# Norm means from float32r pairs, and squares of the first feed-forward nets kept for VectorE

## The chip, the cores and the metric

One Trainium2 chip, one of its cores. The metric is the device time of one execution in microseconds (us): the median of several runs, 2788.34 for the kernel before.

## The reference, cut to what matters

Two blocks run one after the other on x of 512 tokens by 1024 features, all in float32. The first has two layers of an attention mixer and a feed-forward net with a squared relu; the second has a state space block, two gated convolutional nets ("second nets" here) and an attention of another kind. What the change touches is the norm ahead of each of these parts:

```python
def rmsnorm(x, g):
    xf = x.astype(jnp.float32)
    y = xf * lax.rsqrt(jnp.mean(xf * xf, axis=-1, keepdims=True) + EPS)
    return (y * g.astype(jnp.float32)).astype(x.dtype)
...
    for l in range(DEPTH):
        u = rmsnorm(x, pre_mix_g[l])
        m = token_mixer(u, ...)
        x = x + rmsnorm(m, post_mix_g[l])
        h = rmsnorm(x, pre_ffn_g[l]) @ w_ffn_up[l]
        f = jnp.square(jax.nn.relu(h)) @ w_ffn_down[l]
        x = x + rmsnorm(f, post_ffn_g[l])
```

Inside each mixer two more such norms are taken, over 384 and over 256 features.

## The kernel before, in words

**Layout.** Activations lie with features on the 128 partitions and the 512 tokens along the columns, so x is eight tiles of 128 x 512. A float32 value that goes into a product is held as two float32r parts, hi (rounded, written by ScalarE) and lo (the rest, written by VectorE); a product of two such values is three float32r products (hi by hi, hi by lo, lo by hi), `mm3`. Weights come from DRAM in units of 128 x 1024 (SP's queue, `raw`), and are split into `wh` (ScalarE, L230) and `wl` (VectorE, L233). Four buffers hold each of raw, wh and wl. Three short-lived pools matter: 16 tiles of 128 x 512 (s2), 24 of twice that (s4), and 8 banks of PSUM.

**A norm.** The gain is multiplied into x while it is split (xg, L571 and L360), and the division by the root of the mean square is put off: it is multiplied in when a product is taken out of PSUM. The mean square over features is a sum over partitions and tiles. `sq_acc` (L395) squares each tile on ScalarE (L402) and adds the squares into `acc`: for half-width columns on GpSimd (L411, L414), for whole ones on GpSimd too except the first and the last. The eighth tile's square stays apart as `sq`. `mean_mm` (L416) multiplies a matrix of equal constants by acc, and by sq where there is one, in float32, and `rstd` makes the factor from it: three steps on ScalarE (L368, L376, L377), two on VectorE (L384, L388).

**A boundary.** `boundary` (L546) ends a part: for one half of the columns after the other it multiplies the part's result (pn, L567), adds it to x (xr, L568), makes xg's two parts and squares x. The products of the next part begin meanwhile: `lead_group` (L424) runs its first three or four output tiles together, one tile of x after the other, again half by half. It ends with pre(), which issues the mean and the factor; four slots later the tiles are taken out of PSUM by evac. Behind the lead group the other tiles follow one by one (24 products each), for the first nets eight up-tiles and then eight down-tiles, four times over. The norm factor `rr` is first used by `ht` (L591) in a first net, by `z` (L811) in a mixer, by `u` (L1390) in the state space block. There u goes to DRAM and comes back in another order as U, and `vps` are the products with U.

**Order.** The program is a list of closures (`plan`), in the state space block and the attentions by an order written out by hand. `later(n, fn)` issues fn once products of n slots more have been issued; a slot is 512 columns in float32r, and a float32 product counts four. From the instructions so issued a scheduler makes the order of each engine's queue, by priority (earlier issued first) among those that are ready; `pin` keeps an instruction behind all that its engine has been given. Around a lead group the weight splits are pinned: splits of new units wait until 22 closures of the lead group are through, and are pinned for 30 more.

**Which means there are.** Over the whole width twelve: one ahead of each of the two mixers, the two first nets, the state space block, the two second nets and the last attention, and two inside each mixer. Of these the first five named have acc and sq, the others only acc. Ten more run over half the columns, inside the four boundaries and at the end of the kernel.

Of the kernel before, what the change touches and what calls it, by code (L numbers as in the profile page):

```python
# [6 lines left out]
F32 = mybir.dt.float32  # L7
F32R = mybir.dt.float32r
AF = mybir.ActivationFunctionType
ALU = mybir.AluOpType  # L10
AX = mybir.AxisListType

D = 1024
# [94 lines left out]
class Kernel:  # L108
# [21 lines left out]
    LAG = 3  # L130
    LD = 2
# [28 lines left out]
    # ---------------------------------------------------------------- tiles  # L160
# [20 lines left out]
    # -------------------------------------------------------------- weights  # L181
# [14 lines left out]
    def split_early(self, h):  # L196
        """half of the first three units"""
# [40 lines left out]
    def weight(self, u, a, m):  # L238
        """columns a .. a + m of both parts of a unit"""
        hi, lo, w = self.whl[u]  # L240
        i, o = divmod(a, w)
        return hi[i][:, o:o + m], lo[i][:, o:o + m]
# [50 lines left out]
    def later(self, n, fn):  # L293
        """emit fn once n more slots (of 512 columns) of products have been emitted"""
        self.queue.append((self.clock + n, fn))
# [10 lines left out]
    # ------------------------------------------------------------- matmuls  # L306
# [7 lines left out]
    def pin(self, ins):  # L314
        """ins stays behind what its engine has been given so far"""
        self.tc.keep_in_program_order(ins)

    def mm_tok(self, out, x, t, u, a, first, last, n=256):
        """out [128 tokens of tile t, n] += x[:, tokens].T @ W[columns a .. a + n of a unit], in three float32r passes"""
# [14 lines left out]
    def mm3(self, ps, u, k0, nk, kt, m0, m, xs, first, last, ncol=None, cols=ALL):  # L334
        """ps += W[k-tiles, cols].T @ x over nk k-tiles, in three float32r passes."""
# [10 lines left out]
    def split(self, dst, src, scale=None, gain=None):  # L346
        """dst[:,0] + dst[:,1] = src (times scale or a per-partition gain)."""
# [14 lines left out]
    def ln(self, out, in_, load=True, **kw):  # L362
        """Ln from the table set that has Exp too; load: unless it is there already."""
# [6 lines left out]
    def rstd_a(self, v, l=None, cols=ALL, load=True):  # L370
        """v: mean square, the same in all the rows it is used for (PSUM)."""
# [8 lines left out]
    def rstd_b(self, vyq, name="r", cols=ALL, r=None, pin=False):  # L380
        """one Newton step; the result is -2 / sqrt(v + eps): y * ((v + eps) * y * y - 3)"""
# [12 lines left out]
    # ------------------------------------------------------- generic phases  # L394
    def sq_acc(self, st, src, i, n, scale=1.0, cols=ALL, pin=False, one=False):  # L395
        """running sum of squares over tiles; the last stays apart."""
# [26 lines left out]

    def lead_group(self, units, n, xs, evac, st, ones="ones_d", pre=None, mid=None, feed=None):  # L424
        """The first n output tiles k-tile by k-tile, so that the products start with the first tile of x;
        mid: the two halves of the columns one after the other, with mid() once the first has begun."""
        pss = []

        def emit(k, cols, last):
# [4 lines left out]
            if last and k == KT - 1:  # L434
                if pre is not None:
                    pre()
                    self.later(4, lambda: [evac(j, pss[j]) for j in range(n)])
# [34 lines left out]
    def half_tiles(self, units, xs, nk, evac, js, fin):  # L472
        """the last output tiles, the two halves of the columns one after the other; fin() in the second"""
# [24 lines left out]
    # ================================================================ setup  # L498
# [37 lines left out]
    def begin_norm(self, gain, xs, st):  # L536
        """split x * gain, and start the sum of squares of x: a closure for each tile."""
# [8 lines left out]
    def boundary(self, f, st, gain, nxt, res):  # L546
        """x += the norm of f; then begin_norm of the next norm; the closures for the two halves of the columns."""
# [13 lines left out]
        def tile(h, i):  # L561
            cols = HALVES[h]
            xs = res["xs"]
            if i < KT:
# [7 lines left out]
                self.sq_acc(res["st"], x, i, KT, cols=cols)  # L572
# [4 lines left out]
    # ================================================================= FFN  # L577
    def ffn1(self, l, xs, st, nxt, mid, bg=None, last=(), feed=None):
# [7 lines left out]
        def pre():  # L586
            st["r"] = self.rstd(self.mean_mm(st, self.const("ones_d")), "rr", load=False)

        def up(j, ps):
            t = self.s2("ht")  # L590
# [52 lines left out]
    # =============================================================== mixer  # L643
# [9 lines left out]
    def head_norm(self, z, gain, then, n1, n2):  # L653
        """rms norm over the 64 rows of each head, times gain; then(result)."""
# [17 lines left out]
    def v_tiles(self, vf, vst):  # L672
        """v feature-major [two heads of 64, tokens] -> vst [token, tile, head, (hi | lo)]."""
# [8 lines left out]
    def stack(self, dst, src, scale=None):  # L682
        """src [two heads of 64, S] -> dst[h] with hi and lo stacked on the partitions."""
# [11 lines left out]
    def dup(self, dst, src, scale=None):  # L695
        """src [two heads of 64, S] -> dst[h] [128, (hi, lo), S], each on both halves of the partitions."""
# [13 lines left out]
    def softmax_ops(self, name, qk, vst, ydst, spill=None):  # L710
        """The parts of a softmax attention over 8 heads in blocks of 128 queries, by name; a block (h, qt) is 4 h + qt.
        q: scores, e: exponentials, n: division by the sum, t: transposes, p: product with the values, two blocks at once.
        qk(h, qt, ps): scores. vst(h): [128, 4, 128] (hi | lo). ydst: pairs of heads -> hi/lo tiles."""
# [69 lines left out]
    def chunks(self, unit, xs, nk, evac, j, n, m0=0, ncol=None, k0=0):  # L783
        """one output tile as n closures, for use between other work."""
# [14 lines left out]
    def mixer(self, l, xs, st, nxt, mid, feed=None):  # L799
# [6 lines left out]
        def pre():  # L806
            st["r"] = self.rstd(self.mean_mm(st, self.const("ones_d")), "rr", load=False)
# [59 lines left out]
        def ev_c(which, n):  # L867
            def f(j, ps):
# [3 lines left out]
                if j == n - 1:  # L872
                    self.later(18, mean)

            def mean():
                a = self.rstd_a(self.mean_mm(cst[which], self.const("ones_" + which)))
# [16 lines left out]
        def kr_mm():  # L893
            """the products of both parts of w_kr with hi in one pass, one below the other"""
# [26 lines left out]
        # ---- grouped-query attention  # L921
# [1135 lines left out]
```

## Time and profile before

| | us |
|---|---|
| median of three runs | 2788.34 (2786.98 to 2790.88) |
| the profiled execution, first to last instruction | 2786.1 |
| TensorE busy | 2722.6 |
| VectorE busy | 1846.5 |
| ScalarE busy | 1305.1 |
| GpSimd busy | 293.4 |

The profiled execution is known by its span alone; 2.2 us lie between it and the median of the runs. TensorE's matmuls are pipelined and their ends are modelled, so its busy time is an upper bound of what it must spend. PE is TensorE's matmul and PEld its weight load, DVE is VectorE, ACT ScalarE, POOL GpSimd. A row that begins with a time gives start, length, engine, line, operation, the tile written and those read, and shapes; in brackets stands how long the engine had been idle, and who ended it. The mean granted clock of TensorE is 0.989 of its full speed over the span.

### The profile page before, as it was taken

Reading aid. Unit: us, or ns where it says so; the run is one execution under the profiler, and the core shown is the slowest. Engines: PE = TensorE matmul, PEld = TensorE weight load, DVE = VectorE, ACT = ScalarE, POOL = GpSimd, SP = SyncE. Lnnn points to the kernel's source line nnn. Section 1 sums busy time; section 2 is a strip of 40 time slices with the busy share of each in tenths; the row PEclk is TensorE's granted clock in tenths of the full one; section 3 lists DMA queues with packets and bytes.
Section 4 is the critical chain, followed back from the end, with each engine's and each line's share of the span. In section 5 each row is a group of like instructions: output and inputs, shape, how many; then the busy total and the mean of one; then the engine's idle time right before and its main releaser. Section 6 shows DMA issues by size and latency. Waiting matters only on the chain.

```text
span 2786.1 us, 35356 instructions
## 1 busy us (share of the span) xinstructions
PE 2722.6 (98%) x13470; PEld 2268.2 (81%) x13470; DVE 1846.5 (66%) x2963; ACT 1305.1 (47%) x2204; POOL 293.4 (11%) x311
## 2 busy tenths in 40 slices
PE   8999999999999999999999989999999999999998
PEld 6888888888878888888887887888887888888887
DVE  7889863444687996787745784656466667574654
ACT  6567553333465664532334214423236888542333
POOL 1000020000210101121002000101012111110101
PEclk9999999999999999999999879999999999999999
DMA  5323333333232334354445623233324223233331
GB/s 206 116 79 91 121 119 97 95 98 98 96 109 86 93 95 161 110 190 153 137 123 180 183 88 117 91 99 98 99 85 131 68 69 103 84 98 99 98 92 61
DMA packets 122651, 307.47 MB, mean 110 GB/s; under 512 B 35824, under 2 KB 42736, under 8 KB 122352
## 3 DMA queue, kind: packets, MB, share of 16 engines
q1 hardware_dynamic: 109424, 291.57, 32.7%
q10 hardware_dynamic: 10624, 8.39, 1.0%
q0 software_dynamic: 2432, 5.25, 0.9%
q8 instruction: 106, 1.74, 0.3%
q14 instruction: 65, 0.53, 0.1%
HBM read 260.59 MB, written 41.68 MB: 108 GB/s over the span
## 4 chain that ended last, share of the span: by engine, by line
PE 58%; DVE 5%; ACT 1%; issue 1%; DMA 0%; POOL 0%; SPq 0%; DVEq 0%; ACTq 0%; POOLq 0%
PE mm L312 49%; PE z L312 3%; PE yps L312 2%; PE o L312 1%; PE s L312 1%; PE vps L312 1%; DVE xg L360 0%; DVE wl L233 0%; PE gps L312 0%; PE pT L328 0%; DVE pn L567 0%; PE mean L312 0%; DVE xr L568 0%; DVE VS L1431 0%; PE gps L328 0%
## 5 line engine op out<-in xcount | busy, mean ns | idle before, releaser
L312 PE MATMUL mm<-xg,wh 128*128 128x512 f32 (+1 forms) x4080 | 1227.5, 383 | 26.6 <-DVE xg L360 15.5
L312 PEld LDWEIGHTS mm<-xg,wh 128*128 128x128 f32 x4080 | 745.4, 188 | 188.0 <-DVE xg L360 24.6
L230 ACT ACTIVATE wh<-raw 128x1024 fp32r<-128x1024 f32 (+2 forms) x417 | 431.1, 1039 | 830.0 <-PE mm L312 527.5
L312 PE MATMUL mm<-xg,wl 128*128 128x512 f32 (+1 forms) x2024 | 759.5, 378 | 0.0
L233 DVE TENSOR_TENSOR wl<-raw,wh 128x1024 fp32r<-128x1024 f32 (+2 forms) x417 | 531.3, 1278 | 161.9 <-ACT wh L230 156.7
L312 PE MATMUL mm<-hid,wh 128*128 128x512 f32 (+1 forms) x1816 | 539.1, 380 | 0.7 <-DVE hid L357 0.4
L312 PEld LDWEIGHTS mm<-xg,wl 128*128 128x128 f32 x2024 | 381.7, 189 | 71.6 <-issue 0.2
L312 PEld LDWEIGHTS mm<-hid,wh 128*128 128x128 f32 x1816 | 335.0, 188 | 67.0 <-DVE hid L357 1.2
L312 PE MATMUL mm<-hid,wl 128*128 128x512 f32 (+1 forms) x908 | 343.9, 379 | 0.0
L312 PE MATMUL mm<-yhl,wh 128*128 128x512 f32 x640 | 207.3, 403 | 8.7 <-ACT yhl L1494 4.7
L414 POOL TENSOR_TENSOR acc<-acc,sq 128x256 f32<-128x256 f32 (+1 forms) x90 | 106.6, 1185 | 953.1 <-ACT sq L402 952.5
L312 PEld LDWEIGHTS mm<-hid,wl 128*128 128x128 f32 x908 | 170.8, 188 | 31.8
L312 PEld LDWEIGHTS mm<-yhl,wh 128*128 128x128 f32 x640 | 120.1, 192 | 34.6 <-DVE yhl L1495 5.7
L1582 POOL TENSOR_TENSOR gt<-gt,cv 128x512 f32<-128x512 f32 x44 | 74.9, 1703 | 592.7 <-ACT wh L230 471.1
L312 PE MATMUL mm<-yhl,wl 128*128 128x512 f32 x320 | 127.1, 397 | 0.0
L591 DVE SCALAR_TENSOR_TENSOR ht<-mm,rr 128x512 f32<-128x512 f32 x64 | 43.8, 690 | 117.1 <-PE mm L312 116.8
L1590 DVE SCALAR_TENSOR_TENSOR xr<-mm,xr 128x512 f32<-128x512 f32 (+1 forms) x50 | 33.5, 670 | 125.3 <-PE mm L312 125.3
L607 DVE TENSOR_TENSOR part<-part,mm 128x512 f32<-128x512 f32 (+1 forms) x52 | 33.5, 644 | 113.9 <-PE mm L312 113.8
L1570 DVE SCALAR_TENSOR_TENSOR gt<-mm,rr 128x512 f32<-128x512 f32 x88 | 60.6, 690 | 69.6 <-PE mm L312 69.5
L722 DVE TENSOR_REDUCE nm<-s 128x1 f32<-128x512 f32 x128 | 86.4, 680 | 20.8 <-PE s L312 20.4
L749 ACT ACTIVATE pt<-pT 128x512 fp32r<-128x512 f32 x128 | 74.6, 594 | 46.2 <-PE pT L328 45.0
L729 ACT ACTIVATE p<-s,nm 128x512 f32<-128x512 f32 x128 | 87.1, 684 | 11.0 <-DVE nm L722 8.9
(297 smaller groups left out, 3463.5 us busy)
## 6 DMA issues: line engine op xcount, KB each, us to landing
raw<-in_w_up SPq DMA_DIRECT2D x152, 512.0 KB, 3.6
raw<-in_w_down SPq DMA_DIRECT2D x96, 512.0 KB, 3.5
raw<-in_w_in SPq DMA_DIRECT2D x51, 512.0 KB, 3.6
xd<-xr SPq DMA_DIRECT2D x16, 512.0 KB, 2.8
gd<-z SPq DMA_DIRECT2D x32, 256.0 KB, 2.2
g<-gd SPq DMA_DIRECT2D x32, 256.0 KB, 3.9
raw<-in_w_o SPq DMA_DIRECT2D x16, 512.0 KB, 3.6
raw<-in_w_glu SPq DMA_DIRECT2D x16, 512.0 KB, 4.3
```

Source lines behind the costliest of these rows:

```text
L230: ins = self.nc.scalar.activation(h, x, AF.Copy)
L233: ins = lo_engine.tensor_tensor(l, x, h.bitcast(F32), ALU.subtract)
L312: return self.nc.tensor.matmul(out, lhsT, rhs, **kw)
L414: eng.tensor_tensor(st["acc"][:, cols], st["acc"][:, cols], sq[:, cols], ALU.add)
L591: nc.vector.scalar_tensor_tensor(t, ps, 0.0, st["r"], op0=ALU.max, op1=ALU.mult)
L607: nc.vector.tensor_tensor(p, p, ps[:, cols], ALU.add)
L722: nc.vector.tensor_reduce(nm, ps, AX.X, ALU.max, negate=True)
L729: nc.scalar.activation(p, ps, AF.Exp, bias=nm, accum_out=sm)
L749: nc.scalar.activation(hi[:, :, q0:q0 + 128], v, AF.Copy)
L1570: v.scalar_tensor_tensor(t, ps, -0.5, st["r"], op0=ALU.mult, op1=ALU.mult)
L1582: nc.gpsimd.tensor_tensor(t, t, sg.pop(n), ALU.mult)
L1590: v.scalar_tensor_tensor(x, ps[:, cols], 0.5, x, op0=ALU.mult, op1=ALU.add)
```

## The change

1. `sum_split` and `mean_r` are new. The first completes acc on VectorE (adding sq, or the kept squares), scales it by -1/n and splits it into a float32r pair (ScalarE, then VectorE). The second multiplies the pair by a float32r matrix of -1: two products.
2. Seven of the eight norms ahead of a part, and the four inside the mixers, use them. The last attention, the boundaries' own means and the end of the kernel keep the float32 form.
3. At the end of a lead group `sum_split` is issued at once, the mean 10 slots later, or 32 in the first nets, and evac 4 slots after that. Tiles of a first net that finish before the factor is issued wait in a list.
4. In the two boundaries in front of a first net (keep=True) `square` keeps all eight squares, two in s2 tiles and six in three s4 tiles; nothing is added on GpSimd there. `sum_split` adds them on VectorE over all 512 columns.

```diff
+    PRE = 10
+    PRE2 = 32
...
+    def sum_split(self, st, n):
+        v = self.nc.vector
+        if "sqs" in st:
+            st["acc"] = self.s2("acc")
+            v.tensor_tensor(st["acc"], st["sqs"][0], st["sqs"][1], ALU.add)
+            for t in st["sqs"][2:]:
+                v.tensor_tensor(st["acc"], st["acc"], t, ALU.add)
+        elif "sq" in st:
+            v.tensor_tensor(st["acc"], st["acc"], st["sq"], ALU.add)
+        st["hl"] = self.s4("mhl")
+        self.split(st["hl"], st["acc"], scale=-1.0 / n)
+
+    def mean_r(self, st):
+        v = self.ps("mean")
+        for i in range(2):
+            self.mm(v, self.ones_r, st["hl"][:, i], start=i == 0, stop=i == 1)
+        return v
...
             if last and k == KT - 1:
                 if pre is not None:
-                    pre()
-                    self.later(4, lambda: [evac(j, pss[j]) for j in range(n)])
+                    self.sum_split(st, D)
+
+                    def rest():
+                        pre()
+                        self.later(4, lambda: [evac(j, p) for j, p in list(enumerate(pss)) + st.pop("pend", [])])
+                    self.later(self.PRE2 if "sqs" in st else self.PRE, rest)
...
+    def square(self, st, src, i, cols):
+        sqs = st.setdefault("sqs", [])
+        if len(sqs) <= i:
+            if i < 2:
+                sqs.append(self.s2("sq"))
+            else:
+                t = self.s4("sq4", F32)
+                sqs.extend(t[:, k] for k in range(2))
+        self.nc.scalar.activation(sqs[i][:, cols], src, AF.Square)
...
-                self.sq_acc(res["st"], x, i, KT, cols=cols)
+                if keep:
+                    self.square(res["st"], x, i, cols)
+                else:
+                    self.sq_acc(res["st"], x, i, KT, cols=cols)
...
         def pre():
-            st["r"] = self.rstd(self.mean_mm(st, self.const("ones_d")), "rr", load=False)
+            st["r"] = self.rstd(self.mean_r(st), "rr", load=False)
 
         def up(j, ps):
+            if "r" not in st:
+                st.setdefault("pend", []).append((j, ps))
+                return
...
                 if j == n - 1:
+                    self.later(6, lambda: self.sum_split(cst[which], 128 * n))
                     self.later(18, mean)
 
             def mean():
-                a = self.rstd_a(self.mean_mm(cst[which], self.const("ones_" + which)))
+                a = self.rstd_a(self.mean_r(cst[which]))
...
-        fin = self.boundary(lambda i: m[i // 2][:, i % 2], fst, f"post_mix{l}", nxt, res)
+        fin = self.boundary(lambda i: m[i // 2][:, i % 2], fst, f"post_mix{l}", nxt, res, True)
```

The same edit of pre() stands in the mixer, the state space block and the second nets. The rest of the diff takes comments away.

## Rows read from the trace of the kernel before

**Rows 1.** The page, busy us, share of the span and instructions of each engine:

```profile
PE 2722.6 (98%) x13470; PEld 2268.2 (81%) x13470; DVE 1846.5 (66%) x2963; ACT 1305.1 (47%) x2204; POOL 293.4 (11%) x311
```

**Rows 2.** The chain that ended last: start, length, what:

```profile
1158.74 1.72 PE mean L312 x4
...
1767.60 0.86 PE mean L312 x2
1768.46 310.14 PE mm L312 x1368
```

**Rows 3.** Windows over both boundaries ahead of a first net; clock, DMA, GB/s last:

```profile
380.00:411.00 31.00, 27.41 (x199) 24.75 (x198) 26.67 (x51) 16.53 (x40) 10.57 (x12) 1.00 0.12 35
...
1128.00:1159.00 31.00, 27.40 (x198) 24.73 (x198) 26.67 (x51) 16.55 (x39) 10.55 (x12) 1.00 0.28 103
```

**Rows 4.** Waits of PEld, 380:411, then 1128:1159: us, times, longest:

```profile
PEld mm L312 <- DVE xg L360: 5.2, 10, 1.3
PEld mm L312 <- ACT xg L571: 0.8, 2, 0.6
...
PEld mm L312 <- DVE xg L360: 5.1, 10, 1.3
```

**Rows 5.** Groups by line and form, VectorE, 376:412: busy us, mean ns:

```profile
L360 DVE SCALAR_TENSOR_TENSOR xg<-xr,cols,xg 128x256 fp32r<-128x256 f32 x16 | 10.4, 657 | 1.4 <-ACT xg L571 1.4
L567 DVE SCALAR_TENSOR_TENSOR pn<-m,cols,rr 128x256 f32<-128x256 f32 x16 | 8.7, 542 | 0.0
L568 DVE TENSOR_TENSOR xr<-xr,pn 128x256 f32<-128x256 f32 x16 | 8.0, 502 | 0.5
```

**Rows 6.** Timeline, VectorE and GpSimd in the first of these boundaries:

```profile
381.83 0.48 DVE L567 SCALAR_TENSOR_TENSOR pn<-m,cols,rr 128x256 f32<-128x256 f32 x1
382.35 0.43 DVE L568 TENSOR_TENSOR xr<-xr,pn 128x256 f32<-128x256 f32 x1
...
383.77 0.88 POOL L414 TENSOR_TENSOR acc<-acc,sq 128x256 f32<-128x256 f32 x1 [0.40 <-ACT sq L402]
384.08 0.85 DVE L568 TENSOR_TENSOR xr<-xr,pn 128x256 f32<-128x256 f32 x1
```

**Rows 7.** Instructions of tile acc: ns min/median/max, first and last start:

```profile
L411 DVE TENSOR_TENSOR acc<-sq x13: 678/683/693, 9.8 to 2750.0; 128x512 f32<-128x512 f32 x13
```

**Rows 8.** Timeline around the end of that lead group, all engines:

```profile
406.92 1.35 DVE L360 SCALAR_TENSOR_TENSOR xg<-xr,cols,xg 128x256 fp32r<-128x256 f32 x2
...
409.67 2.95 ACT L230 ACTIVATE wh<-raw 128x1024 fp32r<-128x1024 f32 x3 [1.82 <-PE mm L312]
...
410.68 1.02 PE L312 MATMUL mean<-acc,consts 128*128 128x512 f32 x2
...
410.76 3.50 DVE L233 TENSOR_TENSOR wl<-raw,wh 128x1024 fp32r<-128x1024 f32 x3 [2.49 <-ACT wh L230]
...
416.16 1.29 DVE L591 SCALAR_TENSOR_TENSOR ht<-mm,rr 128x512 f32<-128x512 f32 x2
416.88 0.63 ACT L593 ACTIVATE hid<-ht 128x512 fp32r<-128x512 f32 x1 [2.21 <-DVE ht L591]
```

**Rows 9.** Timeline, the first scores of mixer 0 and of mixer 1:

```profile
58.93 1.41 DVE L693 SCALAR_TENSOR_TENSOR qs<-qro,qs 64x512 fp32r<-64x512 f32 x2
...
60.72 0.61 PE L312 MATMUL s<-kk,qs 128*128 128x512 f32 x2
...
809.20 1.41 DVE L693 SCALAR_TENSOR_TENSOR qs<-qro,qs 64x512 fp32r<-64x512 f32 x2
...
809.94 1.16 PE L312 MATMUL s<-kk,qs 128*128 128x512 f32 x2 [5.26 <-DVE qs L693]
```

**Rows 10.** Timeline, the state space block's second u and second vps:

```profile
1549.10 1.11 DVE L1390 SCALAR_TENSOR_TENSOR u<-mm,rr 128x512 f32<-128x512 f32 x1
...
1558.45 1.97 PE L312 MATMUL vps<-U,wt 128*128 128x64 f32 x16 [1.23 <-issue]
```

**Rows 11.** A window over the attentions of mixer 0, columns as in rows 3:

```profile
60.00:340.00 280.00, 278.76 (x1490) 235.08 (x1489) 245.05 (x445) 177.09 (x334) 15.95 (x18) 1.00 0.33 101
```

More of the change, by code (lines that the diff above doesn't have):

```diff
@@ L544, in begin_norm, with boundary @@
         return [lambda i=i: f(i) for i in range(KT)]
-    def boundary(self, f, st, gain, nxt, res):
+    def square(self, st, src, i, cols):
[7 more added lines that the diff above has]
+        self.nc.scalar.activation(sqs[i][:, cols], src, AF.Square)
+    def boundary(self, f, st, gain, nxt, res, keep=False):
         nc = self.nc
@@ L806, in pre @@
         def pre():
-            st["r"] = self.rstd(self.mean_mm(st, self.const("ones_d")), "rr", load=False)
+            st["r"] = self.rstd(self.mean_r(st), "rr", load=False)
         def scaled(ps, rows=128):
@@ L1385, in pre @@
         def pre():
-            st["r"] = self.rstd(self.mean_mm(st, self.const("ones_d")), "rr", load=False)
+            st["r"] = self.rstd(self.mean_r(st), "rr", load=False)
         def ev_u(i, ps):
@@ L1564, in pre @@
         def pre():
-            st["r"] = self.rstd(self.mean_mm(st, self.const("ones_d")), "rr")
+            st["r"] = self.rstd(self.mean_r(st), "rr")
         def up(j, ps):
```

## The prediction, made before the changed kernel ran

> **What bounds the kernel now.** I read the busy table first: TensorE is busy 98% of the span, VectorE 66%, ScalarE 47%, GpSimd 11% [rows 1]. So time goes down in two ways only: fewer TensorE cycles, or fewer of the 63.5 us (2786.1 less 2722.6) in which TensorE waits. Next, the chain of waits: it shows TensorE's true pace, because ends of matmuls are modelled in the other views. 1368 float32r products of 512 columns take 310.14 us, 0.227 us each; a full-width mean takes 1.72 us in four pieces where acc and sq are two products, 0.86 us in two pieces where there is only acc [rows 2]. The granted clock is 1.00 around the first feed-forward nets [rows 3], the 2.4 GHz level, so no term below is a matter of the clock. Then the stretch in which a boundary and the lead group behind it overlap: in 31 us TensorE is busy 27.4, VectorE 26.7 [rows 3]. The waits of the weight loads name who is late: VectorE's xg, ten times, 5.2 us in one net and 5.1 in the other [rows 4]. VectorE is late because of GpSimd. The groups of VectorE there have means of 657, 542 and 502 ns [rows 5], but the same operations also come at 0.43 us alone and 0.85 when an add of the squares is running on GpSimd [rows 6].
>
> **Part 1, the products of the mean.** Eleven of the twelve full-width means become two float32r products, 2 x 0.227 = 0.45 us. Five had two float32 products (both mixers, both first nets, the state space block): 1.72 - 0.45 = 1.27 saved each, 6.35. Six had one (both second nets, two in each mixer): 0.86 - 0.45 = 0.41 each, 2.46. All lie in TensorE's queue between products that are ready, so the sum is **-8.8 us** if nothing is given back.
>
> **Part 2, the adds taken off GpSimd.** Each boundary before a first net loses 12 GpSimd adds (six in each half). On VectorE 16 xg, 16 pn and 16 xr average 657, 542 and 502 ns; undisturbed they come at some 475, 475 and 425 [rows 5, 6]. That is 16 x (0.18 + 0.07 + 0.08) = 5.3 us, 0.44 an add. What of it reaches TensorE is bounded below by nothing (its waits could come from ScalarE's xg next) and above by the 5.2 us of waits on VectorE [rows 4]. The longest of these, 1.3, lies behind a weight split and an add that stays, so 3.9 is what the change can touch. VectorE's step for a tile would be 0.475 + 0.425 + 0.475 = 1.4 us, TensorE's 12 products of 256 columns 12 x 0.227 / 2 = 1.36: nearly even, so I take 3.5 for each net, **-7.0 us**. By the Trainium skill (SBUF — State Buffer, section "SBUF: two separate sides") VectorE and GpSimd share a port pair as an exclusive lock: whoever starts first has it for its whole instruction. By that rule the xr of [rows 6] would have run 0.42 from GpSimd's end at 384.65, to 385.07; it ended at 384.93, so the trace agrees in kind and makes it a little milder. By the rule the 12 adds would cost 6.8 us, and the same share of it would make this term -9.0.
>
> **Part 3, the adds put on VectorE.** Seven adds of 512 columns (0.683 us each [rows 7], about 0.62 apart as the two ht show, 1.29 for two [rows 8]) and the low half of the pair, 0.69: some 5 us of VectorE, with a copy like that of hid, 0.63, on ScalarE [rows 8]. They start when the last xg is through, 408.27, which is 2.4 us before the lead group's end at 410.68 (call it T) [rows 8]. Queued behind them, because weight splits are kept in program order, are the three splits now at 409.67 and 410.76. The fifth unit would be split after 7 x 0.62 + 0.63 + 1.0 + 1.2 = 7.2 us, at T + 4.8. TensorE wants it after the 24 products of the next tile, T + 5.45. Slack 0.65, and more if VectorE is done sooner. I take **0**; if the adds begin only at T, TensorE waits 7.2 - 5.45 = 1.75 us in each net. Weight loads issued by SP move with these splits, but they fetch units four ahead, some 20 us off: no cost.
>
> **Part 4, the later evacuation in the first nets.** The mean moves 36 products past T, so ht starts near T + 12 instead of T + 5.5. Six tiles wait by then: 6 x (0.65 + 0.69) = 8 us of VectorE, and with the later two tiles and two splits 13.2 us, to T + 25.5. The last chunk of the first down product wants the seventh hid at T + 26.3. Banks of PSUM: four, two tiles, the mean and the tile in work are eight of eight. Cost **0**, at worst 2 us in each net.
>
> **Part 5, what the other stages give back.** With 10 slots the evacuation is emitted after 18 products and the short mean, T + 4.5 us, instead of after the long mean and 6 products, T + 3.1: the norm is 1.45 us later, while TensorE is 1.27 earlier. In mixer 1 TensorE already waits 5.26 us for the queries qs before the first scores; in mixer 0 the queries land 0.38 us before them (58.93 + 1.41 against 60.72) [rows 9]. Both waits grow with the 2.7 us: +2.7 and +2.3, **+5.0 us**. Bounds: 0, if VectorE's own queue and not the norm orders the queries, to +5.3 more, a second wait like mixer 1's. In the state space block the second vps waits 1.23 us for U, whose u left VectorE at 1549.10, behind a weight split [rows 10]; this chain through two DMAs (the ACT queue's store, SP's load) does not get earlier, so the 1.27 is lost there, **+1.3** (0 to +2.7). The four means inside the mixers add 0.69 of VectorE and 0.63 of ScalarE each where VectorE is busy 245 of 280 us [rows 11]: **+0.8** for all, between 0 and 4 x 0.69 = 2.8. The added VectorE add at the ends of the other lead groups is one of 0.68, in idle time before T: 0.
>
> **The sum.** -8.8 - 7.0 + 5.0 + 1.3 + 0.8 = -8.7 us. The profiled execution spans 2786.1 us, 2.2 under the median of 2788.34, and I put the sum on the median: **2779.6 us**. About 0.2% (5.6 us) is what a measurement of this kernel can tell from no change.
>
> **Rivals.**
> - *The relief never reaches TensorE.* ScalarE's xg or its wait for the mean of the boundary (0.8 us of waits today, [rows 4]) becomes the bound as VectorE gets faster. For: VectorE's step and TensorE's are nearly even. Against: ScalarE has 16.5 of 31 us busy [rows 3]. Then -8.7 + 7.0: 2786.6.
> - *The sums become the new wait* (slower). The adds of the first seven tiles are ready before the last xg are; if VectorE's order puts six of them, 3.7 us, ahead of the last low halves, TensorE waits for these as it waits now, the second half's relief of 1.75 goes, and the fifth unit's split is late by 1.4. Each net loses 6.85, both 13.7: +5.0, 2793.3. It decides once VectorE has less than 3.7 us free before T. Against it: the adds are issued after the steps they would overtake.
> - *The mixers give nothing back.* VectorE is nearly always busy before the first scores; if the order of its queue is what makes the queries late, the 5.0 goes: 2774.6.
>
> **How the numbers follow.** Forecast 55% (its own range 2775 to 2785), relief lost 17%, sums as a wait 13%, mixers unharmed 15%. The range 2772 to 2790 takes in the forecast, the first and third rival and the lower bounds, and leaves out most of the second. Faster by over 0.2%: most of the forecast and the third rival, 0.62. Within: the rest of the forecast, the first rival, part of the second, 0.26. Slower: 0.12.
>
> **What would show it.** Right: no GpSimd acc in the two stretches of [rows 3], xg, pn and xr near 475, 475 and 425 ns, waits of the weight loads on xg under 2 us, that stretch 4 to 5 us shorter with the mean, TensorE going on through the fifth tile without a gap. In mixer 1 a wait for qs of 8 us or so, in mixer 0 one of 2. Wrong: a gap in front of tile 5, or first scores that are not later; a faster VectorE with the same waits would make the first rival true.

## The result, and the profile after

The change makes the kernel slower: 2807.35 us, the median of four runs (2806.70 to 2809.39), against 2788.16 for the kernel before in the same series (2786.98 to 2790.88). The ratio is 1.0065, 95% interval 1.0053 to 1.0078. Forecast were 2779.6 us and a range up to 2790.

The profiled execution spans 2806.1 us, 20.0 more than the one before. The boundaries' own means (two in each of the four boundaries) are in both kernels and cut the two spans at the same work. The last column is the length of a stretch after less its length before, from the starts of the first half's means in the timeline of TensorE (the last stretch ends with the mean at the end of the kernel):

| stretch | before, us | after, us | after less before |
|---|---|---|---|
| start to the end of mixer 0 | 374.83 | 382.74 | +7.9 |
| first net 0 | 360.33 | 355.41 | -4.9 |
| mixer 1 | 387.58 | 396.89 | +9.3 |
| first net 1 | 381.67 | 376.84 | -4.8 |
| second block (state space block onward) | 1265.57 | 1278.31 | +12.7 |

Both first nets gain what was forecast, 4.77 us each: 1.27 for the mean and 3.5 for VectorE. The loss is in the mixers and in the second block. The page's busy table (first row) and the windows over both boundaries ahead of a first net answer to [rows 1] and [rows 3]; columns as there:

```profile
PE 2725.4 (97%) x13460; PEld 2277.3 (81%) x13460; DVE 1848.8 (66%) x2991; ACT 1308.6 (47%) x2213; POOL 279.0 (10%) x287
...
388.00:419.00 31.00, 29.32 (x216) 27.59 (x216) 27.93 (x61) 18.15 (x41) 0.00 (x0) 1.00 0.16 46
...
1141.00:1172.00 31.00, 29.25 (x214) 27.62 (x214) 27.77 (x60) 17.46 (x39) 0.00 (x0) 1.00 0.34 119
```

TensorE's busy time over the whole span did not fall although products were taken away; its ends are modelled, and a lower clock lengthens it (below). In 31 us at the boundary TensorE now runs 216 matmuls in the first stretch and 214 in the second, instead of 199 and 198, and GpSimd does nothing. The weight loads' waits in 388:419 and VectorE's groups in 384:420 answer to [rows 4] and [rows 5]:

```profile
PEld mm L314 <- DVE xg L362: 1.8, 3, 1.3
...
PEld mm L314 <- ACT xg L607: 0.8, 2, 0.6
```

```profile
L362 DVE SCALAR_TENSOR_TENSOR xg<-xr,cols,xg 128x256 fp32r<-128x256 f32 x16 | 7.7, 481 | 2.8 <-ACT xg L607 2.8
L603 DVE SCALAR_TENSOR_TENSOR pn<-m,cols,rr 128x256 f32<-128x256 f32 x16 | 7.6, 503 | 0.0
L604 DVE TENSOR_TENSOR xr<-xr,pn 128x256 f32<-128x256 f32 x16 | 6.7, 421 | 0.1
```

Waits on xg fell from 5.2 to 1.8 us, and the means from 657, 542 and 502 ns to 481, 503 and 421. The chain of waits gives the short mean as forecast, 0.47 us where [rows 2] have 1.72:

```profile
1175.61 0.47 PE mean L314 x2
```

**Where mixer 0 and mixer 1 lose 8 us each: the mean over the queries inside them.** The timeline of the kernel after in mixer 0, all engines, shortened to the steps that bear on it:

```profile
174.50 0.68 DVE L416 TENSOR_TENSOR acc<-acc,sq 128x512 f32<-128x512 f32 x1
...
178.23 2.09 POOL L691 TENSOR_TENSOR rp<-z,cs 32x512 f32<-32x512 f32 x1 [96.89 <-DVE z L950]
...
180.97 0.68 DVE L693 TENSOR_TENSOR krr<-rp,sh 32x512 f32<-32x512 f32 x1
...
181.69 0.63 ACT L358 ACTIVATE krhl<-krr 32x512 fp32r<-32x512 f32 x1 [1.99 <-DVE krr L693]
182.22 0.61 ACT L355 ACTIVATE mhl<-acc 128x512 fp32r<-128x512 f32 x1
...
182.89 1.59 PE L314 MATMUL mean<-mhl,ones_r 128*128 128x512 f32 x2 [5.46 <-ACT mhl L355]
```

The sum acc is done at 175.18, but its high half mhl starts at 182.22. In ScalarE's queue krhl stands in front of it, the high half of the rotated keys, which waits for a rotation on GpSimd (2.09 us) and two more steps on VectorE. ScalarE is idle for 1.99 us for krhl and does not take mhl meanwhile, though acc has long been done. TensorE has the mean next and waits 5.46 us. Before, the float32 mean took acc directly and ran at 177.22. In mixer 1 the same row stands at 934.39, also with 5.46. Across this mean TensorE falls back against the kernel before by 8.2 us in mixer 0 and by 7.9 in mixer 1: the wait, the low half that comes 0.7 later, the attention steps that both had held up, and TensorE's clock. During the wait the granted clock falls to the lower of its two levels, 1.2 GHz (0.50, third from the end), for 6.8 us; before the change it is 1.00 all through these attentions of mixer 0 [rows 11]. Half of 6.8, 3.4 us, is the most that this can cost (an estimate). The window after in mixer 0; 932.7:939.5 in mixer 1 is at 0.50 too:

```profile
181.80:188.60 6.80, 5.71 (x15) 4.12 (x16) 4.96 (x11) 4.06 (x7) 0.00 (x0) 0.50 0.03 11
```

**Where the second block loses 12.7 us: u's way through DRAM in the state space block.** First TensorE's waits there, before in 1535:1635 and after in 1540:1640 (us, times, longest):

```profile
PE yps L312 <- DVE VS L1431: 3.2, 1, 3.2
PE vps L312 <- issue: 1.2, 1, 1.2
PE vps L312 <- DVE u L1390: 0.7, 1, 0.7
```

```profile
PE yps L314 <- DVE VS L1474: 5.6, 1, 5.6
PE vps L314 <- DMA U<-ud: 4.2, 1, 4.2
PE vps L314 <- DVE u L1433: 3.3, 1, 3.3
PE mm L314 <- DVE xg L362: 0.5, 2, 0.4
```

That is 13.6 us after against 5.1 before (the profile puts a wait for several things down to the one that came last). The chain of waits of the kernel after says what the first vps waits for, and SP's DMA queue (start, length, what it issues) what is in the way:

```profile
1553.63 1.14 DVE u L1433
...
1554.79 7.22 DMA ud<-u
...
1562.06 2.66 DMA U<-ud
...
1564.76 3.69 PE vps L314 x16
```

```profile
1538.79 0.42 SPq L1414 DMA_DIRECT2D wt<-wd  x1
1540.54 0.33 SPq L1416 DMA_DIRECT2D tt<-td  x1
1549.15 3.47 SPq L195 DMA_DIRECT2D raw<-in_w_glu  x3
1552.67 0.42 SPq L1414 DMA_DIRECT2D wt<-wd  x1
1553.19 0.38 SPq L1416 DMA_DIRECT2D tt<-td  x1
```

u's store into DRAM takes 7.22 us; before, U's load was issued 3.8 us after the store (1546.31 and 1550.13). Five loads of 512 KB have been issued in the 5.6 us ahead of it. Two of them, the second pair of the operators wt and tt, had been issued long before the first u in the kernel before, at 1533.03 and 1536.42. The pair mhl takes one of the 24 double-size tiles, those in which wt and tt lie, so their loads are issued later. The factor's steps also take longer: by the chain of waits u starts 5.3 us after the mean's last product ends (1548.29 to 1553.63), 3.6 before (1541.56 to 1545.15), since a weight split now stands between them on either engine. The mean itself ends earlier than before, so that the first u comes only 1.0 us later, counted from the start of the table's last stretch (41.75 us, before 40.74).

The third u loses more, 9.2 us by the same count (1571.24 after, 1554.54 before), by its place in the queues. ScalarE before, then ScalarE and SP after:

```profile
1552.30 1.06 ACT L230 ACTIVATE wh<-raw 128x1024 fp32r<-128x1024 f32 x1 [4.38 <-PE mm L312]
...
1556.98 0.59 ACT L1404 COPY VS<-vps 128x512 f32<-128x512 f32 x1 [3.62 <-PE vps L312]
```

```profile
1568.47 0.32 SPq L1414 DMA_DIRECT2D wt<-wd  x1
1568.48 0.59 ACT L1447 COPY VS<-vps 128x512 f32<-128x512 f32 x1 [12.04 <-PE vps L314]
1568.88 0.38 SPq L1437 DMA_DIRECT2D U<-ud  x1
1569.01 1.06 ACT L232 ACTIVATE wh<-raw 128x1024 fp32r<-128x1024 f32 x1
```

The third u follows in VectorE's queue on the low half of the weights that are split here. Before, ScalarE split them ahead of VS, the copy of the first vps. After, it idles for 12.04 us for VS and splits them behind it. In SP's queue the second load of U stands behind a load of wt that is issued when the first vps ends; before, U's came first (1555.40, wt at 1556.97).

By the Trainium skill (DMA: Bandwidth & Descriptors, section "Issuing engines are not separate DMA queues") DMAs that different engines issue run on the same DMA engines and interleave. The trace agrees: a store from ScalarE's queue took 7.2 us behind SP's loads.

The rest goes with TensorE's clock. Windows of 20 us over the block, the granted clock third from the end; before, then after:

```profile
1600.00:1620.00 20.00, 20.00 (x96) 20.00 (x95) 18.37 (x55) 2.44 (x4) 0.00 (x0) 0.50 0.58 192
1620.00:1640.00 20.00, 20.00 (x145) 18.73 (x145) 15.57 (x36) 5.30 (x9) 0.00 (x0) 0.94 0.12 36
```

```profile
1607.00:1627.00 20.00, 20.00 (x96) 20.00 (x95) 15.78 (x31) 3.68 (x5) 0.00 (x0) 0.50 0.36 83
1627.00:1647.00 20.00, 20.00 (x87) 18.95 (x87) 17.43 (x58) 4.68 (x8) 0.00 (x0) 0.52 0.45 154
```

Both kernels are at the lower level here, behind the wait for VS (3.2 us, over at 1587.07, and 5.6, over at 1600.71). Before, the next window is back at 0.94, with 145 matmuls; after, it is still at 0.52, with 87. Over the whole stretch (1540:1700 before, 1547:1720 after) the mean granted clock is 0.85 and 0.78.

### The profile page after: what moved, and what is told of

The parts are those of the page before. It is cut to its first block, busy times and chain, and to the rows that moved or that the text cites. A ratio compares the mean times of both kernels' runs of the same rounds, so it can differ in the third digit from the quotient of the medians.

```text
span 2806.1 us, 35328 instructions
## 1 busy us (share of the span) xinstructions
PE 2725.4 (97%) x13460; PEld 2277.3 (81%) x13460; DVE 1848.8 (66%) x2991; ACT 1308.6 (47%) x2213; POOL 279.0 (10%) x287
## 3 DMA queue, kind: packets, MB, share of 16 engines
HBM read 260.59 MB, written 41.68 MB: 108 GB/s over the span
## 4 chain that ended last, share of the span: by engine, by line
PE 57%; DVE 4%; ACT 2%; DMA 1%; issue 1%; POOL 0%; SPq 0%; DVEq 0%; ACTq 0%; POOLq 0%
PE mm L314 49%; PE z L314 3%; PE yps L314 2%; PE o L314 1%; PE vps L314 1%; PE s L314 1%; DVE wl L235 0%; PE gps L314 0%; PE pT L330 0%; DVE xg L362 0%; DMA g<-gd 0%; DVE VS L1474 0%; DMA ud<-u 0%; DVE pn L603 0%; PE gps L330 0%
## 5 line engine op out<-in xcount | busy, mean ns | idle before, releaser
L416 POOL TENSOR_TENSOR acc<-acc,sq 128x512 f32<-128x512 f32 (+1 forms) x70 | 89.3, 1275 | 968.9 <-ACT sq L404 856.5
L1625 POOL TENSOR_TENSOR gt<-gt,cv 128x512 f32<-128x512 f32 x44 | 80.9, 1840 | 585.9 <-ACT wh L232 449.7
L792 DVE TENSOR_TENSOR pt<-pT,pt 128x512 fp32r<-128x512 f32 x128 | 86.7, 684 | 12.3 <-ACT pt L791 11.4
```

Of the source, the lines that this page charges most:

```text
L416: eng.tensor_tensor(st["acc"][:, cols], st["acc"][:, cols], sq[:, cols], ALU.add)
L792: nc.vector.tensor_tensor(lo[:, :, q0:q0 + 128], v, hi[:, :, q0:q0 + 128].bitcast(F32), ALU.subtract)
L1625: nc.gpsimd.tensor_tensor(t, t, sg.pop(n), ALU.mult)
```

## The experiments

Theory A, formed from the two traces: the two losses are apart from each other. In the mixers it is the place of mhl in ScalarE's queue; in the state space block the tile that mhl takes, and the later factor. Theory B: the pairs are dear everywhere, because they add work to VectorE and ScalarE. Ten kernels were run; each ratio is to runs of the kernel before in the same series. The stretch lengths, less those of the kernel before, come from the one profiled execution of each (us):

| kernel | mixer 0 | net 0 | mixer 1 | net 1 | second block | ratio, 95% |
|---|---|---|---|---|---|---|
| after | +7.9 | -4.9 | +9.3 | -4.8 | +12.7 | 1.0065 (1.0053 to 1.0078) |
| e1_inner_f32 | +0.4 | -4.8 | +1.9 | -4.9 | +14.0 | 1.0011 (1.0001 to 1.0021) |
| e2_ssm_f32 | +6.9 | -4.9 | +9.6 | -4.9 | +0.2 | 1.0016 (1.0005 to 1.0026) |
| e3_both_f32 | +0.2 | -4.8 | +3.7 | -4.9 | -0.2 | 0.9970 (0.9957 to 0.9983) |
| e4_ssm_s2 | +6.2 | -4.9 | +8.6 | -4.9 | +7.2 | 1.0042 (1.0026 to 1.0058) |
| e10_ssm_s2_now | +7.5 | -4.9 | +10.0 | -4.9 | +3.6 | 1.0023 (1.0008 to 1.0039) |
| e6_no_keep | -0.3 | -1.6 | +3.6 | -1.6 | +0.2 | 0.9992 (0.9983 to 1.0001) |
| e8_mixer_f32 | +0.4 | -4.8 | +1.8 | -4.8 | +1.8 | 0.9972 (0.9955 to 0.9988) |
| e9_early_ssmf32 | -1.4 | -4.8 | +2.5 | -4.9 | +10.4 | 0.9966 (0.9956 to 0.9977) |
| e7_pre2_10 | -0.5 | -4.9 | +2.0 | -4.9 | -0.6 | 0.9955 (0.9940 to 0.9970) |
| e11_best | -1.7 | -4.9 | -0.2 | -4.9 | -0.8 | 0.9952 (0.9939 to 0.9964) |

**Which loss is where: e1, e2 and e3.** The four means inside the mixers go back to float32 (e1), the one ahead of the state space block does (e2), or both (e3). The edit of e1, then that of e2, where `mean_r` is `mean_mm` for a norm that has no pair:

```diff
-                    self.later(6, lambda: self.sum_split(cst[which], 128 * n))
...
-                a = self.rstd_a(self.mean_r(cst[which]))
+                a = self.rstd_a(self.mean_mm(cst[which], self.const("ones_" + which)))
```

```diff
-    def lead_group(self, units, n, xs, evac, st, ones="ones_d", pre=None, mid=None, feed=None):
+    def lead_group(self, units, n, xs, evac, st, ones="ones_d", pre=None, mid=None, feed=None, how="r"):
...
-                if pre is not None:
+                if pre is not None and how == "mm":
+                    pre()
+                    self.later(4, lambda: [evac(j, pss[j]) for j in range(n)])
+                elif pre is not None:
                     self.sum_split(st, D)
...
-        self.lead_group([U(i) for i in range(n)], n, lambda: xs, ev_u, st, pre=pre, mid=mid, feed=feed)
+        self.lead_group([U(i) for i in range(n)], n, lambda: xs, ev_u, st, pre=pre, mid=mid, feed=feed, how="mm")
```

> The changed kernel, but the four means inside the mixers are float32 products again. Theory: in each mixer the mean over 384 features waits for the high half of its pair, which stands in ScalarE's queue behind the split of the rotated keys (5.46 us of waiting TensorE shown, some 8 us between matching scores before and after it), so both mixers give back about 16 us: near 2791 us, and no wait of TensorE on a mean. Rival: the waiting mean only shows a VectorE and ScalarE that are overloaded in the attentions; then the wait moves to the next product and less than 8 us come back: 2799 or more.

> The changed kernel, but the state space block's mean is two float32 products at the end of the lead group again. Theory: the 13.6 us lost between that mean and the second nets come from this mean alone, so some 13 us come back: near 2794 us, and the first vps waits for nothing. Rival: they come from the way the stage ahead (the first net of layer 1) hands over its buffers and loads; then under 5 us come back: 2802 or more.

> Both of the above. Theory: the two losses add up, 16 + 13.6 us, and what is left is the gain of the first nets (4.9 and 4.8), 0.4 in each second net, and about 0 over the mixers' lead groups: near 2778 us, faster than the kernel before by some 10. Rival: the losses overlap, and the kernel stays above 2785.

Measured: 2791.99, 2794.14 and 2780.10 us, near the 2791, 2794 and 2778 expected, against 2789.27 before. From the ratios, e1 takes back 0.54% (15 us) of the loss, e2 0.49% (14 us), and both 0.95% (26 us), nearly the sum. So these are two losses, apart, and without them the change is faster by 0.3%. The table has them in the stretches that were named: +7.9 and +9.3 to +0.4 and +1.9 by e1, +12.7 to +0.2 by e2.

**Place in the queue or the work: e9.** The pairs inside the mixers stay, but are issued as soon as acc is, so that mhl stands ahead of krhl; the state space block is as in e2.

```diff
-                    self.later(6, lambda: self.sum_split(cst[which], 128 * n))
+                    self.sum_split(cst[which], 128 * n)
```

> The changed kernel with a float32 mean in the state space block, and inside the mixers the pairs are issued at once when acc is done, ahead of the products for the rotated keys, not six slots later behind them. Theory: what cost 16 us inside the mixers is only the place of the high half in ScalarE's queue; ahead of the rotated keys' split it costs nothing and the short means gain 0.4 each: 2778 to 2780, no wait of TensorE on a mean. Rival: any pair inside the attentions costs (ScalarE and VectorE are full there): 2785 or more.

Measured: 2780.93 us, ratio 0.9966. The timeline of e9 in mixer 0, ScalarE, VectorE and TensorE:

```profile
175.20 0.63 ACT L364 ACTIVATE mhl<-acc 128x512 fp32r<-128x512 f32 x1 [1.44 <-DVE acc L425]
175.87 0.69 DVE L365 SCALAR_TENSOR_TENSOR mhl<-acc,mhl 128x512 fp32r<-128x512 f32 x1
...
176.30 0.39 PE L323 MATMUL mean<-mhl,ones_r 128*128 128x512 f32 x1
```

The same two instructions are there, 7 us earlier, and TensorE waits for neither; the granted clock is 1.00 here. e9 beats e2, which differs from it by this one line, by 0.5%, some 14 us of the 16: the loss came from the place in the queues, and none is seen from the work of the pair. Theory B falls for the mixers.

The second block of e9 needs a word. This profiled execution took 2789.65 us at a mean granted clock of 0.982, the kernel's seven other runs 2778.66 to 2782.72 at 0.985 to 0.987. TensorE's waits in the state space block are 5.2 us in it, as before the change, but late in the block, where the window before the change that answers to it (1660:1680) is at 0.93, the clock is 0.60:

```profile
1651.00:1671.00 20.00, 19.00 (x94) 18.12 (x92) 10.53 (x29) 4.09 (x7) 0.00 (x0) 0.60 0.12 36
```

Over the stretch (1531:1701) the mean clock is 0.78, as in the kernel after. So this block can be some 10 us longer by a lower clock without any more waiting, here in one execution of eight. Differences of a few us in the table's column of the second block are not read for this reason.

**Tile, lateness or work in the state space block: e4 and e10.** In e4 the pair lies in two tiles of the small pool instead of one of the double-size pool. e10 also issues mean and factor at once. Both edits are for this block alone; the last two lines of the diff are in e10 only.

```diff
-        st["hl"] = self.s4("mhl")
-        self.split(st["hl"], st["acc"], scale=-1.0 / n)
+        st["hl"] = [self.s2("mh", F32R), self.s2("ml", F32R)]
+        self.nc.scalar.activation(st["hl"][0], st["acc"], AF.Copy, scale=-1.0 / n)
+        v.scalar_tensor_tensor(st["hl"][1], st["acc"], -1.0 / n, st["hl"][0].bitcast(F32), op0=ALU.mult, op1=ALU.subtract)
...
-                    self.later(self.PRE2 if "sqs" in st else self.PRE, rest)
+                    self.later(self.PRE2 if "sqs" in st else 0, rest)
```

> The changed kernel, but the pair of the state space block's mean lies in two small tiles of the pool of 16, not in one of the pool of 24. Theory: the pair takes the buffer that a pair of operator loads had before, so 1 MB of loads comes in the way of the first u on its way through DRAM; with the small tiles these loads are early again and 8 to 13 us come back: 2794 to 2799. Rival: it is the later factor (mean later, weight splits between its steps) that makes u late; then at most 3 us come back: 2804 or more.

> The changed kernel with the state space block's pair in two small tiles, and its mean issued at the end of the lead group, not 10 slots later. Theory: small tiles alone gave back 7.4 of 13.6 us; the rest is the later factor, so with the mean at once about 5 us more come back: near 2795. Rival: the rest is the pair itself, whose halves stand ahead of the weight splits on ScalarE and VectorE whenever the mean comes: no change against 2800.

Measured: 2799.91 us, just above the theory's 2794 to 2799, and 2797.40, midway between the theory's 2795 and the rival's 2800. SP's queue in e4 has both pairs of operators early again, and SP's load of U follows ScalarE's store of u closely:

```profile
1538.04 0.33 SPq L1437 DMA_DIRECT2D wt<-wd  x1
1541.44 0.33 SPq L1439 DMA_DIRECT2D tt<-td  x1
...
1552.30 0.38 ACTq L1458 DMA_DIRECT2D ud<-u  x1
1554.93 0.33 SPq L1460 DMA_DIRECT2D U<-ud  x1
```

2.6 us lie between them instead of 7.3 after the change and 3.8 before it. By the ratios the tile is worth 0.23% (6.4 us), the 10 slots 0.19% (5.3), and the pair against a float32 mean the remaining 0.07% (2). With intervals of 0.10% to 0.16% to either side, only the first of the three is clear of noise, and barely.

What the 10 slots do is not what the theory of e10 says. In e10 the first u starts as late as in e4 (41.68 and 41.72 us after the start of the table's last stretch), and TensorE waits 0.8 us for the pair's high half ahead of the mean. What comes earlier is the third u (49.9 us, in e4 53.1): in e4 its weight split on ScalarE stands behind VS (1560.32 and 1559.84), in e10 ahead of it (1559.78 and 1564.45), as before the change, and the second load of U is ahead of wt again. This is argued from the order of the rows; no run changes that order alone. e4 still waits 9.9 us in the block (5.7 for VS, 4.0 for u, 0.2 for xg). So the tile of Theory A is shown, its later factor is not, and a remainder of some 2 us may be Theory B's. The weight loads of the vps products (ns, min/median/max) show what waits and clock do together; the kernel after, then e11 below, which has the float32 mean there:

```profile
L314 PEld LDWEIGHTS vps<-U,wt x128: 188/333/334, 1564.8 to 1641.4; 128*128 128x128 f32 x128
```

```profile
L323 PEld LDWEIGHTS vps<-U,wt x128: 186/192/334, 1543.3 to 1606.8; 128*128 128x128 f32 x128
```

With the pair the median load takes 333 ns (in e1, e4 and e10 too), without it 192.

**What the kept squares bring: e6.** e3 with the squares added on GpSimd again, the means still short.

```diff
-        fin = self.boundary(lambda i: m[i // 2][:, i % 2], fst, f"post_mix{l}", nxt, res, True)
+        fin = self.boundary(lambda i: m[i // 2][:, i % 2], fst, f"post_mix{l}", nxt, res, False)
```

> As the kernel with float32 means inside the mixers and in the state space block, but without the kept squares: in front of the first nets GpSimd adds the half-width squares again, the pair is made from acc and sq, and the mean comes 10 slots later. Theory: the relief of VectorE from GpSimd is worth 3.5 us in each first net, the shorter mean 1.27, so 7 us of that kernel's gain go: near 2787 us, and the weight loads wait for VectorE's xg about 5 us in each boundary again. Rival: the gain came from moving the mean and the evacuation out of the way; then it stays within 2 us of 2780.

Measured: 2786.76 us, ratio 0.9992 (e3: 0.9970). Each net keeps only 1.6 of its 4.9 us. VectorE and the weight loads stand where they stood before the change [rows 4, 5]; e6, groups in 376:412:

```profile
L371 DVE SCALAR_TENSOR_TENSOR xg<-xr,cols,xg 128x256 fp32r<-128x256 f32 x16 | 10.4, 657 | 1.4 <-ACT xg L627 1.4
L623 DVE SCALAR_TENSOR_TENSOR pn<-m,cols,rr 128x256 f32<-128x256 f32 x16 | 8.7, 542 | 0.0
L624 DVE TENSOR_TENSOR xr<-xr,pn 128x256 f32<-128x256 f32 x16 | 8.0, 503 | 0.5
```

So 3.2 us of the first and 3.3 of the second net come from taking the adds off GpSimd.

**The lead means of the mixers: e8.** e3 with these two means in float32 as well.

```diff
-        self.lead_group([U(i) for i in range(n)], n, lambda: xs, lead, st, pre=pre, mid=mid, feed=feed)
+        self.lead_group([U(i) for i in range(n)], n, lambda: xs, lead, st, pre=pre, mid=mid, feed=feed, how="mm")
```

> As the kernel with float32 means inside the mixers and in the state space block, with the means ahead of the two mixers in float32 and at once too. Theory: they give 1.7 us in mixer 0, where the first scores don't wait, and take 1.7 in mixer 1, where the wait for the queries grew from 5.26 to 7.6; undone together nothing changes: 2780 within 2 us, and the wait for the queries is 5.3 us again. Rival: the wait of 7.6 us has another origin (the stage ahead), then it stays and 1 to 2 us are lost.

Measured: 2780.13 us, ratio 0.9972: together the two mixers gain nothing. In mixer 0 the first scores are at 61.04 (e3: 59.54), so the short mean gains 1.5 us there, though the table shows only 0.2 of it at the mixer's end; in mixer 1 the wait for the queries is back at 5.28 (after: 7.60). The first scores after, in mixer 0 and in mixer 1, for [rows 9]:

```profile
59.56 0.62 PE L314 MATMUL s<-kk,qs 128*128 128x512 f32 x2
...
814.62 1.22 PE L314 MATMUL s<-kk,qs 128*128 128x512 f32 x2 [7.60 <-DVE qs L735]
```

**The delay of 32 slots: e7.** e3 with 10 slots in the first nets too.

```diff
-    PRE2 = 32
+    PRE2 = 10
```

> The kernel with float32 means in the state space block and inside the mixers, and the first nets' mean 10 slots after the lead group instead of 32. Theory (the seven adds and the pair take VectorE and ScalarE some 5.5 us, and start about 2.4 us before the lead group ends): the mean, 10 products or 2.3 us behind the lead group, waits 1 to 3 us for mhl in each first net, so 2781.5 to 2786 where 32 slots gave 2780.1. Rival (the delay only moves evacuations and is needless): within 1 us of 2780.1, and no wait on mhl.

Measured: 2777.20 us, ratio 0.9955 (e3: 0.9970, the intervals overlap). The price of 1 to 3 us in each net failed; the rival, that the delay is needless and mhl waited for by nobody, holds, though the time lies 2.9 us below its 2780.1, further than the 1 us it named. The timeline of e7 shows why: the adds begin among the last tiles' steps, the last of them ends at 407.16, and the pair is ready before the mean's turn.

```profile
408.21 0.69 DVE L365 SCALAR_TENSOR_TENSOR mhl<-acc,mhl 128x512 fp32r<-128x512 f32 x1
...
409.29 0.63 PE L323 MATMUL mean<-mhl,ones_r 128*128 128x512 f32 x2
```

**The version that keeps the gains: e11.** e9 with mixer 1's lead mean in float32.

```diff
-        self.lead_group([U(i) for i in range(n)], n, lambda: xs, lead, st, pre=pre, mid=mid, feed=feed, how="mm")
+        self.lead_group([U(i) for i in range(n)], n, lambda: xs, lead, st, pre=pre, mid=mid, feed=feed, how="r" if l == 0 else "mm")
```

> The changed kernel with three edits: the state space block's mean and mixer 1's lead mean in float32 as before, and the inner pairs made at once after acc instead of 6 slots later. Theory: what remains is the two first nets (-4.8 each), mixer 0 (about -1.5), the second nets (-0.4 each) and the four inner means (-0.3 to -0.4 each): 2788.2 - 9.6 - 1.5 - 0.9 - 1.4 = about 2775 to 2779, faster than before by over 0.3%; no wait above 0.3 us in front of an inner mean, the queries' wait before mixer 1's first scores back to about 5.3. Rival (the inner pair costs by VectorE's and ScalarE's time, not by its place in the queue): the inner means give back what they save, 2780 to 2782, no better than with float32 inner means.

Measured: 2775.46 us (2772.46 to 2779.38) against 2789.65 before, ratio 0.9952: faster than both kernels, and within what was expected. No mean inside a mixer waits, and the wait ahead of mixer 1's first scores is 5.33. In the table no stretch is longer than before. e11 with e7's 10 slots was not tried.

## Why the prediction was wrong

Four parts held as to their sizes, and two small terms of the fifth were wrong by 16 and by 13 us; together they turned a gain of 8.7 us into a loss.

- **Part 1** held for the price, 0.47 us against 0.45 forecast. Its sentence "All lie in TensorE's queue between products that are ready" was wrong for the pairs: TensorE's products were ready, the mean's own operand was not.
- **Part 2** held: 3.5 us a net forecast, 3.2 and 3.3 by e6. With the mean the nets gain 4.9 and 4.8; 4.77 was forecast. Its means were a little off: pn, taken at 475 ns undisturbed, runs at 503, so VectorE itself gained 16 x (0.176 + 0.039 + 0.082) = 4.8 us, not 5.3. By the rule of the port lock, in the Trainium skill (SBUF — State Buffer, section "SBUF: two separate sides"), the term would have been -9.0 for both nets; it measured -6.5, so these runs are nearer to the figure taken from the rows. The first rival (relief lost) falls.
- **Parts 3 and 4** held: TensorE waits for nothing in 419:470, around the first net's mean and behind it, where a gap ahead of tile 5 had been named as the sign of an error. The second rival (sums as a wait) falls. Its sign, though, is there in small: the first adds do come ahead of the last xg, and cost nothing.
- **Part 5, mixers' lead means.** In mixer 1 the wait rose from 5.26 to 7.60, 2.3 of 2.7 forecast. In mixer 0 the forecast +2.3 did not come: the first scores are 1.16 us earlier, though the factor rr is 1.97 later (32.67, before 30.70). The normed query behind them, qn, is there 3.4 us earlier than before (50.14, before 53.55), and VectorE turns to its rotation only at 54.53, when it is through with the four parts of the keys kk (50.81 to 54.60). So here the order of VectorE's queue sets the queries, and not the factor. The third rival (nothing given back) was right for mixer 0 alone.
- **Part 5, "four inner means: +0.8", bounded by 2.8.** This is the step that failed most: about +16 in its place (8.2 and 7.9, on the two query means; the two others gain 0.3 to 0.4 each). The term counted the pair's 0.69 us of VectorE and 0.63 of ScalarE and bounded the loss by their sum. What counted was what stands ahead of mhl in ScalarE's queue when it is issued 6 slots late, the split of keys that are still being rotated, and the lower clock that the wait brought with it. e9 moves mhl forward and the loss is gone.
- **Part 5, "state space block: +1.3 (0 to +2.7)".** The second step that failed. With the gains of the mean and of the second nets the second block was to be 0.8 us shorter; it is 12.7 longer. The prediction saw that u's chain through DRAM ends last here, and that the norm gets later, but charged only the 1.27 that the mean saves. The first u is 1.0 later, within the 1.45 that it gave the norm. It missed that mhl comes out of the pool of wt and tt (e4: 6.4 us), and that the 10 slots put the third u's weight split and U's second load behind other work in their queues (e10: 5.3, not clear of noise, the way argued). What of this is waiting and what the lower clock is not settled: waits grew by 8.5 us between the two profiled executions, the rest of the 13.5 goes with work at the lower level, and e9 shows that this part changes from one execution to another by itself.

The sum without the two failed terms would have been near: e3, which takes both out, has 2780.1, and the forecast was 2779.6. This agreement is partly luck, as mixer 0 and mixer 1 come out differently from the forecast there. Between e3 and e7, which have the same code in mixer 1, that stretch differs by 1.7 us in one execution each; differences of that size in the table are not read.

## What to carry to other kernels

When a step that was one instruction on one engine becomes two on engines with queues of their own, its price is the wait of whatever stands ahead of it there, not its busy time: look for the instruction in front, and what that one waits for. Look as well at whom a later issue puts behind others: here a weight split and a load of U. Give a new operand a buffer from a pool that nobody fills with prefetches, or count whose load is put off by one place and what that load then runs beside. Taking work off GpSimd next to a busy VectorE paid 3.2 and 3.3 us in the two boundaries here.

## What the runs showed of the hardware that was not expected

- VectorE's xg, pn and xr lose 176, 39 and 82 ns each on average beside GpSimd's adds (657, 542 and 503 ns in e6; 481, 503 and 421 in the kernel after).
- A 256 KB store into DRAM took 7.2 us with 2.5 MB of loads issued in the 5.6 us before it, and the next step was issued 2.6 us after it where two of those five loads had come earlier (e4).
- In each mixer TensorE's clock fell to the lower level within a wait of 5.46 us, and stayed there for 6.8 us in all; without the wait (e9, 176:194 and 920:945) it is 1.00.
- In the state space block waits of a few us go together with a longer stretch at the lower level of TensorE's clock: of the vps weight loads the median is 192 ns before the change and in e11, and 333 ns in the kernel after, e4 and e10. One execution of e9 had 192 and no more waiting, and was longer by 10 us at the lower level all the same.
